# Scan work of VectorE set between projections, two half products of the output in the last chunk of pb, and weight loads in 8 KB rows

## The chip, the cores and the metric

One Trainium2 chip, one core of it. The metric is the device time of one execution in microseconds. The kernel before ran three times: 902.72, 903.78 and 906.15 us, median 903.78.

## What is computed

One encoder block on 256 tokens of width 2048, in float32. The input is normalised, multiplied by one wide matrix (2048 x 13312), and the columns feed a bidirectional linear recurrence (RG-LRU), windowed attention with grouped heads, the gates of both, and two merge gates:

```python
xn = rms_norm(x, norm_pre_w)
z = xn @ w_in
u_lru, g_lru, q, k, v, g_attn, m_lru, m_attn = split(z)
u = centred_depthwise_conv(u_lru, conv_w, conv_b)          # 4 taps
h = rg_lru(u, forward weights) + rg_lru(u, reverse weights)  # h[t] = a[t] h[t-1] + b[t]
y_a = h * silu(g_lru)
y_b = windowed_gqa(rope(q), rope(k), v, sink) * silu(g_attn)
merged = sigmoid(m_lru) * (y_a @ w_proj_a) + sigmoid(m_attn) * (y_b @ w_proj_b)
out = x + rms_norm(merged @ w_out, norm_post_w)
```

## The kernel before, in words

**Products.** Each float32 matrix is used as the sum of a high and a low part. A weight tile comes from DRAM as raw float32, ScalarE (ACT) casts it to the high part `wh` (L230), VectorE (DVE) subtracts that from the raw to get the low part `wl` (L232), and TensorE (PE) makes three products: high by high, low by high, high by low. Where 256 tokens lie side by side, two of them run as one matmul of 512 columns (L263) and the low one as 256 columns (L261); elsewhere all three have 512 columns (L236 to L238, `mm3`).

**Steps and ticks.** The program is a list of steps (`load_plan`), one for each 1 MB of weights (128 x 2048). A step has two halves of 128 x 1024. The kernel is written out half by half: with half `hs`, ACT's cast of half hs+4 and VectorE's split of half hs+3 are issued. The raw tiles of a step are loaded three steps ahead (`fetch`, lead 3). A tick is one half of a normal step or both halves of a `part` step. Everything else hangs on ticks: `at(tick, fn)`, `behind(tick, fn)` (at the end of that tick) and `soon(fn)` (one tick later). The engines each run their instructions in that order, and SP issues nearly all the loads in that order too; a load that must wait for its buffer or its data holds up every load behind it on SP.

**Buffers.** `unit` gives one of UNITS = 50 buffers of 4 KB a partition to everything: raw tiles, wh, wl, activations, gates. A buffer comes free when its last reader is done, whichever engine that is.

**Seven products instead of eight.** Half of the columns of three matrices (groups L, A and O: two merge gates and the output projection) are computed by a Strassen-like scheme of seven products m1 to m7 (`class Seven`), with sums of blocks of activations (`x_sums`, `sums_of`) and sums of blocks of weights. Products m1 and m2 take weights as they are; the others take them from a cell x (m5, then m6, then m4) or y (m3, then m7), in which the next weight block is added onto what is there by an accumulating DMA that POOL issues (L203, queue q0). The next accumulation has to wait until the earlier content is cast and split. In groups L and A the sums of activations are stored to DRAM (`away`, L341) and read back (`Lm`, `Am`, x_sum).

**RG-LRU.** `lru_pair(n, b)` sets the work of two column blocks on ticks from b on: convolution taps (L659), gates, decays, `gi * th` (L726), four scans of 256 steps, two forward and two reverse (L703, L704), `gate_out` (L709, L710) and `y_parts`. The table LRU gives b for each of the eight pairs, XSUM the ticks of the eight `x_sums`.

**The end.** After the projections q, pa, ma and pb (MERGE) comes the output projection (OUT): chunks o2 and o3 as normal steps, the other half as group O (`Om` in the profile). When a chunk of the output is there, `o_done` squares, sums and scales it; at the end the rows of x (`xr`) are added. Weights of the norm are `np`. Attention needs `mask` and `rope`.

The lines that set the order of the tail:

```python
b, n = ticks(), ticks(len(plan))        # b: first tick of OUT, n: last
at(b + 12, load_tail)                   # np
at(n - 6, load_rows)                    # xr
for q in range(2):
    at(b - 16 + 4 * q, lambda q=q: seven.start("x", q))
    at(b - 12 + 4 * q, lambda q=q: seven.second(q))
    at(b - 4 + 4 * q, lambda q=q: seven.start("y", q))
```

Of the kernel before, what the change touches and what calls it, by code (L numbers as in the profile page):

```python
# [29 lines left out]
UNITS = 50  # L30
# [3 lines left out]
G = 1  # L34
# [30 lines left out]
XSUM = (24, 30, 36, 42, 48, 54, 60, 65)  # L65
LRU = (12, 28, 45, 62, 78, 93, 108, 121)
# [62 lines left out]
def body(ctx, tc, x, xT, wall, wlru, pvec, npost, ident_d, mask_d, rope_d, out):  # L129
    nc = tc.nc  # L130
    const = ctx.enter_context(tc.tile_pool(name="const", bufs=1))
    units = ctx.enter_context(tc.tile_pool(name="units", bufs=UNITS))
    small = ctx.enter_context(tc.tile_pool(name="small", bufs=2))
# [136 lines left out]
    def add_rows(name, act, done, spare=False, last=False):  # L270


        got, held = [], []

        def products(t, g, h, wh, wl):
            ts = slice(t * P, (t + 1) * P)
            for j in range(2):
                k = 4 * g + 2 * h + j
                sl = slice(j * 512, (j + 1) * 512)
                a = act[k // 2][:, k % 2, :, ts]  # L280
                mm3(got[t], a[:, 0], a[:, 1], wh[:, sl], wl[:, sl], k == 0, k == KT - 1)

        def half(g, h, wh, wl):
            if g == 0 and h == 0:
                if spare:
# [63 lines left out]
    class Seven:  # L349
# [51 lines left out]
        def half(self, m, q, h, wh, wl):  # L401
            b = {"m6": "m1", "m7": "m1", "m4": "m1", "m3": "m5"}.get(m, m)
# [10 lines left out]
        def keep(self, key, ps):  # L413
            t = self.kept.get("t")
            if key == "u" or t is None:
                t = unit(f"{self.name}{key}", F32, (P, 2, 512))
                if key != "u":
                    self.kept["t"] = t
            self.kept[key] = t[:, int(key == "m5")]
            nc.scalar.copy(self.kept[key], ps)  # L420

        def after(self, m):
# [31 lines left out]
    mask = const.tile([P, 2, S], F32, name="mask")  # L454
    rope = const.tile([ROT, 2, S], F32, name="rope")
# [4 lines left out]
    raw_units(0)  # L460
# [3 lines left out]
    for i in (1, 2):  # L464
        for j in (0, 2):
            nc.sync.dma_start(xt[i][:, j:j + 2], xT[i, :, j:j + 2])
            if j == 0:
                raw_units(i)
# [69 lines left out]

    def load_tables():
        nc.sync.dma_start(mask, mask_d)  # L540
        nc.sync.dma_start(rope, rope_d)

    at(20, load_tables)
# [91 lines left out]
    def lru_pair(n, b):  # L635
# [64 lines left out]
        def scans():  # L700
            a, h, b = v["a"], v["gr"], v["gi"]
            for j in range(2):
                nc.vector.tensor_tensor_scan(h[:, j], a[:, j], b[:, j], 0.0, ALU.mult, ALU.add)  # L703
                nc.vector.tensor_tensor_scan(h[:, 2 + j, ::-1], a[:, 2 + j, ::-1], b[:, 2 + j, ::-1], 0.0, ALU.mult, ALU.add)  # L704
# [25 lines left out]
        at(b + 21 + G, y_parts)  # L730

# [45 lines left out]
    add_ml = lambda c: add_rows(f"ml{c}_", xs, gate_evac(tm, c), c == 0)  # L777
# [19 lines left out]
    swap = [(i + 16) % 32 for i in range(32)]  # L797

    def add_heads(name, then):
# [12 lines left out]
        def rotate(n, d):  # L812
            t = v[n]
            r = t[0:ROT]
            if d == 0:
                v["s"] = small.tile([ROT, 2, S], F32, tag="upad", name=f"{name}s{n}", bufs=2)
                nc.vector.stream_shuffle(v["s"], r, swap)
                nc.vector.tensor_tensor(r, r, rope[:, 0].unsqueeze(1).to_broadcast([ROT, 2, S]), ALU.mult)
            elif d == 1:
                s = v["s"]  # L820
                nc.vector.tensor_tensor(s, s, rope[:, 1].unsqueeze(1).to_broadcast([ROT, 2, S]), ALU.mult)
# [24 lines left out]
    def head(hd, qh, ql, b, both):  # L846
# [11 lines left out]
        def expo():  # L858
# [4 lines left out]
            for t in range(2):  # L863
                nc.vector.tensor_tensor_reduce(p[:, t], sc[:, t], mask[:, t], rtok_sc[:, t:t + 1], sk, ALU.add, ALU.max, m[:, t:t + 1])  # L864
# [59 lines left out]
    def add_pa(c):  # L924
        add_rows(f"pa{c}_", ya, lambda t, ps: nc.vector.tensor_tensor(tm[c][:, t], ps, tm[c][:, t], ALU.mult))
# [39 lines left out]

    tick = add_all(MERGE, lambda kind, c: {
# [4 lines left out]
    }[kind]())  # L971
    for n in range(8):
        at(tick["b0.0"] - 10 + 2 * n, lambda n=n: yb_parts(n))
# [20 lines left out]
    at(b + 12, load_tail)  # L994
    at(n - 6, load_rows)
# [38 lines left out]
    def rows_in_psum():  # L1034

        a, b = banks("xp", (P, 2, 512)), banks("xq", (P, 2, 512))
        xp.update({1: a[:, 0], 3: a[:, 1], 2: b[:, 0]})
# [3 lines left out]
    def o_sum(t, c, ps, other, sign):  # L1041
        if other is None:
            o_done(t, c, ps)
        else:
            f = small.tile([P, 512], F32, tag="p", name=f"of{t}{c}", bufs=2)
# [3 lines left out]
    seven = Seven("O", ms, msum, o_sum)  # L1049
# [4 lines left out]
    add_all(OUT, lambda _, c: add_rows(f"o{c}_", ms, lambda t, ps: o_done(t, c, ps), c == 3, c == 3))  # L1054
# [98 lines left out]
```

## Time and profile before

| | |
|---|---|
| median of three runs | 903.78 us |
| the profiled execution | 906.24 us |
| its span, first to last instruction | 904.5 us |
| granted TensorE clock, mean | 0.993 |
| TensorE busy | 889.1 us |
| VectorE busy | 699.3 us |
| ScalarE busy | 597.6 us |
| moved by DMA | 205.80 MB, mean 228 GB/s |

Times in the profile are microseconds from the start of the span. In lists of waits each row names who waited for whom, then the total, how often, and the longest. In timelines a row gives the start, the duration, the engine, the line and what was written from what; in square brackets stands the idle time ahead of it and what ended that.

### The profile page before, as it was taken

Reading aid. Unit: us, or ns where it says so; the run is one execution under the profiler, and the core shown is the slowest. Engines: PE = TensorE matmul, PEld = TensorE weight load, DVE = VectorE, ACT = ScalarE, POOL = GpSimd, SP = SyncE. Lnnn points to the kernel's source line nnn. Section 1 sums busy time; section 2 is a strip of 40 time slices with the busy share of each in tenths; the row PEclk is TensorE's granted clock in tenths of the full one; section 3 lists DMA queues with packets and bytes.
Section 4 is the critical chain, followed back from the end, with each engine's and each line's share of the span. In section 5 each row is a group of like instructions: output and inputs, shape, how many; then the busy total and the mean of one; then the engine's idle time right before and its main releaser. Section 6 shows DMA issues by size and latency. Waiting matters only on the chain.

```text
span 904.5 us, 12540 instructions
## 1 busy us (share of the span) xinstructions
PE 889.1 (98%) x4590; PEld 760.2 (84%) x4590; DVE 699.3 (77%) x958; ACT 597.6 (66%) x869; POOL 44.7 (5%) x72
## 2 busy tenths in 40 slices
PE   8999999998999999999999999999999999999996
PEld 8888888887888888898888888888888888888865
DVE  6887999798897979798657768586666678668584
ACT  7689695867878788975454555455696565446572
POOL 0000000100010100000000000000001200001100
PEclk9999999999999999999999999999999999999989
DMA  9953476985898956545554554556959987965992
GB/s 326 409 198 111 140 283 214 345 253 193 249 255 304 247 195 219 201 163 209 183 204 150 186 166 139 178 169 215 269 160 323 296 273 221 351 267 140 274 328 96
DMA packets 61646, 205.80 MB, mean 228 GB/s; under 512 B 6512, under 2 KB 11376, under 8 KB 61584
## 3 DMA queue, kind: packets, MB, share of 16 engines
q1 hardware_dynamic: 54096, 179.07, 55.4%
q0 software_dynamic: 6912, 25.17, 14.6%
q8 instruction: 36, 0.59, 0.3%
q10 hardware_dynamic: 576, 0.76, 0.3%
q14 instruction: 26, 0.21, 0.1%
HBM read 198.68 MB, written 6.29 MB: 227 GB/s over the span
## 4 chain that ended last, share of the span: by engine, by line
PE 88%; DMA 6%; DVE 3%; issue 2%; ACT 1%; POOLq 0%; ACTq 0%; SPq 0%; DVEq 0%
PE q L263 6%; PE ga L263 6%; PE gl L263 6%; PE u L263 4%; DMA raw<-wall_dram 4%; PE q L261 3%; PE ga L261 3%; PE gl L261 3%; PE u L261 2%; PE k L263 2%; PE Am L236 1%; PE Am L237 1%; PE Am L238 1%; PE u_ps L555 1%; PE Lm L237 1%
## 5 line engine op out<-in xcount | busy, mean ns | idle before, releaser
L232 DVE TENSOR_TENSOR wl<-raw,wh 128x1024 fp32r<-128x1024 f32 (+1 forms) x276 | 327.7, 1203 | 67.7 <-ACT wh L230 58.0
L230 ACT CAST wh<-raw 128x1024 fp32r<-128x1024 f32 (+1 forms) x275 | 276.2, 1038 | 54.6 <-DMA raw<-wall_dram 33.5
L263 PE MATMUL ga<-xs,wh 128*128 128x512 f32 x256 | 64.2, 398 | 0.0
L263 PE MATMUL q<-xs,wh 128*128 128x512 f32 x256 | 62.8, 391 | 0.0
L263 PE MATMUL gl<-xs,wh 128*128 128x512 f32 x256 | 62.4, 391 | 0.0
L263 PEld LDWEIGHTS ga<-xs,wh 128*128 128x128 f32 x256 | 47.9, 193 | 9.3
L263 PEld LDWEIGHTS gl<-xs,wh 128*128 128x128 f32 x256 | 47.0, 188 | 9.0
L263 PEld LDWEIGHTS q<-xs,wh 128*128 128x128 f32 x256 | 46.6, 188 | 8.8
L263 PE MATMUL u<-xs,wh 128*128 128x512 f32 x192 | 46.8, 391 | 0.0
L160 ACT CAST ph<-pt 128x512 fp32r<-128x512 f32 x16 | 9.4, 586 | 55.2 <-PE pt L884 55.2
L263 PEld LDWEIGHTS u<-xs,wh 128*128 128x128 f32 x192 | 35.2, 188 | 6.7
L261 PE MATMUL ga<-xs,wl 128*128 128x256 f32 x256 | 34.8, 285 | 2.8 <-DVE wl L232 2.8
L261 PEld LDWEIGHTS ga<-xs,wl 128*128 128x128 f32 x256 | 33.3, 191 | 4.8 <-DVE wl L232 3.6
L261 PE MATMUL q<-xs,wl 128*128 128x256 f32 x256 | 34.4, 284 | 0.0
L261 PEld LDWEIGHTS q<-xs,wl 128*128 128x128 f32 x256 | 33.1, 191 | 1.3
L261 PEld LDWEIGHTS gl<-xs,wl 128*128 128x128 f32 x256 | 32.9, 191 | 1.2
L261 PE MATMUL gl<-xs,wl 128*128 128x256 f32 x256 | 33.4, 283 | 0.0
L864 DVE CUSTOM_DVE_ANT_0 p<-sc,mask,pv 128x256 f32<-128x256 f32 x32 | 16.1, 540 | 18.7 <-PE sc L238 18.7
L261 PEld LDWEIGHTS u<-xs,wl 128*128 128x128 f32 x192 | 24.7, 191 | 0.9
L261 PE MATMUL u<-xs,wl 128*128 128x256 f32 x192 | 25.1, 283 | 0.0
L659 DVE SCALAR_TENSOR_TENSOR uu<-upad,pv,uu 128x256 f32<-128x256 f32 x48 | 23.1, 481 | 1.9 <-ACT uu L655 0.2
L160 ACT CAST ms<-mt 128x512 fp32r<-128x512 f32 x8 | 4.7, 588 | 28.5 <-PE mt L942 28.5
(495 smaller groups left out, 2200.6 us busy)
## 6 DMA issues: line engine op xcount, KB each, us to landing
raw<-wall_dram SPq DMA_DIRECT2D x268, 512.0 KB, 5.8
lraw<-wlru_dram SPq DMA_DIRECT2D x8, 512.0 KB, 6.7
away<-xx SPq DMA_DIRECT2D x8, 512.0 KB, 4.1
Lm<-away SPq DMA_DIRECT2D x8, 512.0 KB, 7.6
Am<-away SPq DMA_DIRECT2D x8, 512.0 KB, 10.6
raw<-wall_dram SPq DMA_DIRECT2D x8, 256.0 KB, 4.8
xr<-x_dram SPq DMA_DIRECT2D x4, 512.0 KB, 9.6
Lx0a<-wall_dram POOLq DMA_DIRECT2D x3, 512.0 KB, 8.7
```

The source lines that it names most:

```text
L160: nc.scalar.copy(h, src)
L230: cast(hs, raw)
L232: nc.vector.tensor_tensor(ls, raw, hs.bitcast(F32), ALU.subtract)
L236: nc.tensor.matmul(ps, wh, xh, start=start, stop=False, skip_group_check=more)
L237: nc.tensor.matmul(ps, wh, xl, start=False, stop=False, skip_group_check=more)
L238: nc.tensor.matmul(ps, wl, xh, start=False, stop=stop, skip_group_check=more)
L261: nc.tensor.matmul(ps[:, 1], wl[:, sl], a[:, 0], start=False, stop=False)
L263: nc.tensor.matmul(ps, wh[:, sl], a, start=k == 0, stop=k == KT - 1)
L555: nc.tensor.matmul(ups[b // 2][:, b % 2, m], w[:, sl], a[:, n], start=k == 0 and w is wh and m == 0, stop=stop)
L659: nc.vector.scalar_tensor_tensor(u, up[:, j, tap:tap + S], cw[:, tap:tap + 1], u, ALU.mult, ALU.add)
L864: nc.vector.tensor_tensor_reduce(p[:, t], sc[:, t], mask[:, t], rtok_sc[:, t:t + 1], sk, ALU.add, ALU.max, m[:, t:t + 1])
```

## The change

1. The work of a pair of the RG-LRU after the decays moves to later ticks and is spread: `gi * th` at +19 (17 before), two scans at +21 and two at +24 (all four at +18 before), gate_out at +28 (20), y_parts at +29 (22). LRU changes by one or two ticks for some pairs, XSUM runs from 20 to 55 in steps of 5 (24 to 65 in steps of mostly 6).
2. Raw weight tiles come from a pool of their own, three tiles of 1 MB, each loaded by one DMA with rows of 8 KB instead of two with rows of 4 KB. UNITS goes from 50 to 45.
3. Om1.0 and Om5.0 move into pb's last chunk, and the rest of OUT is reordered. Group O's first x loads start at b-22 and b-14, their second content at b-18 and b-10, its y loads at b-2 and b+2. `np` is loaded at b-8 and `xr` at b-4.
4. m4 gets a PSUM bank of its own in groups A and O: m7's bank is copied aside (`keep("w")`, one ACT copy), and for m4 a combination on VectorE adds it.
5. Gates of the merge wait in DRAM for their use (`park`, four stores of 512 KB, and `back`, four loads). `mask` and `rope` are loaded into a unit six ticks ahead of the heads. `yb_parts` are spread by 1.5 instead of 2 ticks from b0-4 (b0-10 before). Chunk o3 and xp use banks of other pools, and o2's `o_done` comes one and two ticks later.

```diff
-UNITS = 50
+UNITS = 45
...
-G = 1
...
-    b0.3 Am6.1 b1.0 b1.1 Am7.0 b1.2 Am7.1 b1.3 b2.0 Am4.0 b2.1 Am4.1 b2.2 b2.3 b3.0 b3.1 b3.2 b3.3""".split()
-OUT = """o2.0 Om1.0 o2.1 Om1.1 o2.2 Om5.0 Om5.1 o2.3 Om3.0 Om3.1 Om6.0 Om6.1 o3.0 Om2.0 Om2.1 Om7.0 Om7.1 o3.1
-    Om4.0 Om4.1 o3.2 o3.3""".split()
+    b0.3 Am6.1 b1.0 b1.1 Am7.0 b1.2 Am7.1 b1.3 b2.0 Am4.0 b2.1 Am4.1 b2.2 b2.3 b3.0 Om1.0 b3.1 Om5.0 b3.2 b3.3""".split()
+OUT = """o2.0 o2.1 Om1.1 o2.2 Om5.1 Om2.0 o2.3 Om3.0 Om6.0 Om3.1 o3.0 Om6.1 Om2.1 o3.1 Om7.0 Om7.1 Om4.0 Om4.1
+    o3.2 o3.3""".split()
...
-XSUM = (24, 30, 36, 42, 48, 54, 60, 65)
-LRU = (12, 28, 45, 62, 78, 93, 108, 121)
+XSUM = (20, 25, 30, 35, 40, 45, 50, 55)
+LRU = (12, 28, 45, 64, 79, 94, 109, 121)
...
+    ring = ctx.enter_context(tc.tile_pool(name="ring", bufs=3))
...
-    def raw_units(i):
-        raws[i] = [unit(f"raw{i}_{h}", F32, (P, 1024)) for h in range(2)]
-        return raws[i]
+    def raw_tile(i):
+        t = ring.tile([P, 2, 1024], F32, tag="raw", name=f"raw{i}", bufs=3)
+        raws[i] = [t[:, h] for h in range(2)]
+        return t
...
-            load(raw_units(i), plan[i])
+            nc.sync.dma_start(flat(raw_tile(i)), wall[row[content(plan[i])]])
...
+            self.bank = {"m6": "m1", "m7": "m1", "m4": "m1" if sums is None else "m4", "m3": "m5"}
...
                 done(1, 1, ps["m1"], kept["m5"], -1)
+                if self.bank["m4"] == "m4":
+                    self.keep("w", ps["m1"])
             elif m == "m4":
-                done(1, 0, ps["m1"], None, 1)
+                done(1, 0, ps[self.bank["m4"]], kept.get("w"), 1)
...
-            (10, lambda: decays("th", AF.Tanh, cpos, 0)), (10, lambda: decays("th", AF.Tanh, cpos, 1)), (10, gated),
-            (11, lambda: decays("a", AF.Exp, cneg, 0)), (12, lambda: decays("a", AF.Exp, cneg, 1)),
-            (12, lambda: nc.scalar.activation(v["gr"], v["a"], AF.Square)), (13, scale1),
-            (14, lambda: nc.scalar.activation(v["th"], v["th"], AF.Sqrt)),
-            (16, lambda: nc.vector.tensor_tensor(v["gi"], v["gi"], v["th"], ALU.mult)),
-            (17, scans), (19, gate_out),
+            (10, lambda: decays("th", AF.Tanh, cpos, 0)), (10, lambda: decays("th", AF.Tanh, cpos, 1)), (11, gated),
+            (12, lambda: decays("a", AF.Exp, cneg, 0)), (13, lambda: decays("a", AF.Exp, cneg, 1)),
+            (13, lambda: nc.scalar.activation(v["gr"], v["a"], AF.Square)), (14, scale1),
+            (15, lambda: nc.scalar.activation(v["th"], v["th"], AF.Sqrt)),
+            (19, lambda: nc.vector.tensor_tensor(v["gi"], v["gi"], v["th"], ALU.mult)),
+            (21, lambda: scans(0)), (24, lambda: scans(1)), (28, gate_out), (29, y_parts),
         ):
-            at(b + d + (G if d > 5 else 0), fn)
-        at(b + 21 + G, y_parts)
+            at(b + d, fn)
...
+    def park(gates, c):
+
+        d = parked[c] = dram.tile([P, 1024], F32, name=f"park{c}")
+        nc.sync.dma_start(d, flat(gates.pop(c)))
+
+    def back(gates, c):
+        nc.sync.dma_start(flat(gate_unit(gates, c)), parked[c])
...
-    at(b + 12, load_tail)
-    at(n - 6, load_rows)
+    at(b - 8, load_tail)
+    at(b - 4, load_rows)
...
-        at(b - 16 + 4 * q, lambda q=q: seven.start("x", q))
-        at(b - 12 + 4 * q, lambda q=q: seven.second(q))
-        at(b - 4 + 4 * q, lambda q=q: seven.start("y", q))
+        at(b - 22 + 8 * q, lambda q=q: seven.start("x", q))
+        at(b - 18 + 8 * q, lambda q=q: seven.second(q))
+        at(b - 2 + 4 * q, lambda q=q: seven.start("y", q))
```

How the order of instructions moves, at three places. First VectorE around the scans of the first pair (`gr`, `a`, `gi` belong to the pair, `uu` and `upad` to the convolution of the next one, `wl` are splits of raw weights). Before:

```order
L232 TENSOR_TENSOR wl_0_978<-raw_0_916,wh_0_977 128x1024
L703 SCALAR_TENSOR_TENSOR gr_728<-a_856,gi_729 128x256
L704 SCALAR_TENSOR_TENSOR gr_728<-a_856,gi_729 128x256
L703 SCALAR_TENSOR_TENSOR gr_728<-a_856,gi_729 128x256
L704 SCALAR_TENSOR_TENSOR gr_728<-a_856,gi_729 128x256
L659 SCALAR_TENSOR_TENSOR uu_971<-upad_463,pv,uu_971 128x256 x3
L232 TENSOR_TENSOR wl_1_1006<-raw_1_917,wh_1_1005 128x1024
```

Changed (L701 and L702 are the scans, L233 the split, L343 and L324 to L326 the x sums):

```order
L233 TENSOR_TENSOR wl_1_1041<-raw_945,wh_1_1040 128x1024
L701 SCALAR_TENSOR_TENSOR gr_680<-a_837,gi_681 128x256
L702 SCALAR_TENSOR_TENSOR gr_680<-a_837,gi_681 128x256
L589 TENSOR_TENSOR sg_724<-gl_958,sg_724 128x512
L585 TENSOR_TENSOR sg_724<-sg_724,rbc 128x512
L233 TENSOR_TENSOR wl_0_1066<-raw_1001,wh_0_1065 128x1024
L233 TENSOR_TENSOR wl_1_1092<-raw_1001,wh_1_1091 128x1024
L739 TENSOR_TENSOR sg_724<-sg_724,sig_1127 128x512
L233 TENSOR_TENSOR wl_0_1130<-raw_1060,wh_0_1129 128x1024
```

The four scans stood between two splits; now two stand there, and the other two follow four splits later.

Second, the loads on SP in the first third of the program, with the engines they wait for (DMAHW are earlier DMAs; PE_49 means a wait for TensorE). Before:

```order
L205 DMA raw_0_1206<-wall_dram 128x1024 [waits DMAHW7_49,PE_49]
L205 DMA raw_1_1207<-wall_dram 128x1024 [waits DMAHW0_49,PE_49]
L205 DMA raw_0_1281<-wall_dram 128x1024 [waits DMAHW1_49,PE_49]
L205 DMA raw_1_1282<-wall_dram 128x1024 [waits DMAHW2_49]
L341 DMA away_71<-xx_1223 512x1x256 [waits DMAHW3_49,DVE_49]
```

Changed:

```order
L219 DMA raw_1060<-wall_dram 128x2048 [waits DMAHW6_49,DVE_49]
L344 DMA away_74<-xx_1015 512x1x256 [waits DMAHW3_49,DVE_49]
L219 DMA raw_1111<-wall_dram 128x2048 [waits DMAHW7_49,DVE_49]
L219 DMA raw_1182<-wall_dram 128x2048 [waits DMAHW5_49,DMAHW1_49,DVE_49]
L219 DMA raw_1250<-wall_dram 128x2048 [waits DMAHW2_49,DVE_49]
```

A step is one load instead of two, and it waits for VectorE, the last reader of the ring's tile, where it waited for TensorE, the last reader of a unit's former content.

Third, TensorE in pb's last chunk (`pb` are its products, `Om` those of group O). Before:

```order
L237 MATMUL pb__7428<-wl_1_7363,yb_6459 128x512
L238 MATMUL pb__7428<-wh_1_7362,yb_6459 128x512
L236 MATMUL pb__7428<-wh_0_7382,yb_6523 128x512
L237 MATMUL pb__7428<-wl_0_7383,yb_6523 128x512
L238 MATMUL pb__7428<-wh_0_7382,yb_6523 128x512
```

Changed:

```order
L238 MATMUL pb__7199<-wl_1_7138,yb_6401 128x512
L239 MATMUL pb__7199<-wh_1_7137,yb_6401 128x512
L237 MATMUL Om_7256<-wh_0_7155,ms_6746 128x512
L238 MATMUL Om_7256<-wl_0_7156,ms_6746 128x512
L239 MATMUL Om_7256<-wh_0_7155,ms_6746 128x512
```

After the first step of that chunk the twelve matmuls of Om1.0 now stand, and after its second step those of Om5.0, ahead of the output's own chunks.

More of the change, by code (lines that the diff above doesn't have):

```diff
@@ L284, in half @@
             if g == 0 and h == 0:
-                if spare:
+                if last:
+                    got.extend(banks(f"{name}{t}", (P, 2, 512))[:, 0] for t in range(2))
+                elif spare:
                     got.extend(bank(f"{name}{t}", (P, 512)) for t in range(2))
@@ L401, in half @@
         def half(self, m, q, h, wh, wl):
-            b = {"m6": "m1", "m7": "m1", "m4": "m1", "m3": "m5"}.get(m, m)
+            b = self.bank.get(m, m)
             fresh, last = q == 0 and h == 0 and b == m, q == 1 and h == 1
@@ L459, in body @@
     xs = []
-    raw_units(0)
+    raw_tile(0)
     for j in range(4):
@@ L698, in scale1, with scans @@
             nc.vector.scalar_tensor_tensor(v["th"], v["gr"], 1.0, v["th"], ALU.add, ALU.mult)
-        def scans():
+        def scans(j):
             a, h, b = v["a"], v["gr"], v["gi"]
-            for j in range(2):
-                nc.vector.tensor_tensor_scan(h[:, j], a[:, j], b[:, j], 0.0, ALU.mult, ALU.add)
-                nc.vector.tensor_tensor_scan(h[:, 2 + j, ::-1], a[:, 2 + j, ::-1], b[:, 2 + j, ::-1], 0.0, ALU.mult, ALU.add)
+            nc.vector.tensor_tensor_scan(h[:, j], a[:, j], b[:, j], 0.0, ALU.mult, ALU.add)
+            nc.vector.tensor_tensor_scan(h[:, 2 + j, ::-1], a[:, 2 + j, ::-1], b[:, 2 + j, ::-1], 0.0, ALU.mult, ALU.add)
         def gate_out():
@@ L797, in body, with load_tables @@
     swap = [(i + 16) % 32 for i in range(32)]
+    table = {}
+    def load_tables():
+        t = unit("table")
+        table.update(mask=t[:, 0:2], rope=t[0:ROT, 2:4])
+        nc.sync.dma_start(table["mask"], mask_d)
+        nc.sync.dma_start(table["rope"], rope_d)
+    at(ticks() - 6, load_tables)
     def add_heads(name, then):
@@ L924, in add_pa, with done @@
     def add_pa(c):
-        add_rows(f"pa{c}_", ya, lambda t, ps: nc.vector.tensor_tensor(tm[c][:, t], ps, tm[c][:, t], ALU.mult))
+        def done(t, ps):
+            nc.vector.tensor_tensor(tm[c][:, t], ps, tm[c][:, t], ALU.mult)
+            if t == 1 and c >= 2:
+                soon(lambda: park(tm, c), 2)
+        add_rows(f"pa{c}_", ya, done)
     def add_pb(c):
@@ L964, in add_all @@
         return tick
+    seven = Seven("O", ms, msum, lambda *a: o_sum(*a))
     tick = add_all(MERGE, lambda kind, c: {
@@ L971, in body @@
     }[kind]())
+    for c in range(4):
+        at(tick[f"p{c}.0" if c < 2 else f"b{c}.0"], lambda c=c: back(tm, c))
     for n in range(8):
-        at(tick["b0.0"] - 10 + 2 * n, lambda n=n: yb_parts(n))
+        at(tick["b0.0"] - 4 + 3 * n // 2, lambda n=n: yb_parts(n))
     npt, xr, yw = [], [[], []], [[], []]
@@ L1034, in rows_in_psum @@
     def rows_in_psum():
-        a, b = banks("xp", (P, 2, 512)), banks("xq", (P, 2, 512))
-        xp.update({1: a[:, 0], 3: a[:, 1], 2: b[:, 0]})
+        xp.update({q: bank(f"xp{q}", (P, 512)) for q in (1, 3, 2)})
         for q, to in xp.items():
```

32 lines of the change are left out of this document (16 added, 16 removed).

## The prediction

> **What bounds the kernel now.** I read the page first: busy shares and granted clock.
>
> ```profile
> span 904.5 us, 12540 instructions
> PE 889.1 (98%) x4590; PEld 760.2 (84%) x4590; DVE 699.3 (77%) x958; ACT 597.6 (66%) x869; POOL 44.7 (5%) x72
> PEclk9999999999999999999999999999999999999989
> DMA  9953476985898956545554554556959987965992
> ```
>
> TensorE is busy for 98% of the span, and the change takes no matmul away. So all that can be won lies where TensorE waits or runs at a lower granted clock. The clock shows one dip in 40 slices; TensorE's list of waits, read stretch by stretch, leads to it and to one more place. The table by 5 us stretches shows both (columns: stretch, then length, busy time with the number of instructions of PE, PEld, DVE, ACT, POOL, granted clock, DMA share, GB/s).
>
> ```profile
> 200.00:205.00 5.00, 4.21 (x18) 2.85 (x17) 4.96 (x7) 1.57 (x2) 0.14 (x2) 1.00 0.63 252
> 205.00:210.00 5.00, 2.76 (x18) 2.46 (x19) 4.46 (x8) 3.43 (x6) 0.00 (x0) 0.91 0.00 0
> 210.00:215.00 5.00, 5.00 (x24) 4.24 (x23) 4.96 (x7) 4.97 (x7) 0.00 (x0) 0.74 0.70 188
> ...
> 860.00:865.00 5.00, 3.35 (x13) 1.97 (x11) 2.35 (x3) 2.20 (x5) 1.33 (x2) 0.95 1.05 276
> 865.00:870.00 5.00, 4.54 (x11) 3.37 (x11) 4.67 (x5) 4.80 (x6) 0.00 (x0) 0.50 1.05 273
> 870.00:875.00 5.00, 5.00 (x20) 4.04 (x20) 4.93 (x9) 3.94 (x6) 0.00 (x0) 0.87 1.04 340
> ```
>
> First place: TensorE idle 0.79 + 2.24 = 3.0 us, VectorE full, and DMA at nothing in the middle stretch. Second: idle 1.65 + 0.46 = 2.1 us, DMA at its limit, and the clock at half for a whole stretch. What each costs I take from TensorE's timeline (start, duration, instruction).
>
> ```profile
> 200.16 0.39 PE L238 MATMUL Lm<-wh,xs 128*128 128x512 f32 x1
> 200.39 0.39 PE L236 MATMUL Lm<-wh,xs 128*128 128x512 f32 x1
> 201.22 0.50 PE L237 MATMUL Lm<-wl,xs 128*128 128x512 f32 x1 [0.45 <-DVE wl L232]
> ...
> 202.48 2.00 PE L263 MATMUL ga<-xs,wh 128*128 128x512 f32 x8
> 204.82 1.21 PE L261 MATMUL ga<-xs,wl 128*128 128x256 f32 x8 [0.34 <-DVE wl L232]
> 208.28 1.39 PE L261 MATMUL ga<-xs,wl 128*128 128x256 f32 x8 [2.24 <-DVE wl L232]
> 209.46 3.45 PE L263 MATMUL ga<-xs,wh 128*128 128x512 f32 x8
> 212.75 0.28 PE L236 MATMUL gate<-ul,lwh 128*128 128x256 f32 x1
> 212.87 0.28 PE L237 MATMUL gate<-ul,lwh 128*128 128x256 f32 x1
> ...
> 861.01 0.39 PE L236 MATMUL Om<-wh,ms 128*128 128x512 f32 x1
> ...
> 871.41 0.40 PE L238 MATMUL Om<-wh,mx 128*128 128x512 f32 x1
> 871.65 0.40 PE L236 MATMUL Om<-wh,mx 128*128 128x512 f32 x1
> ```
>
> Unhindered, matmuls of 512 columns start 0.227 us apart (0.23 between the first two rows) and those of 256 columns 0.12. From 200.39 to 212.75 there are 6 of Lm, 16 of L263 and 16 of L261: 22 x 0.227 + 16 x 0.12 = 6.9 us of work in 12.36 us. **Stall 1 costs 5.4 us.** From 861.01 to 871.65 stand 21 matmuls: 21 x 0.227 = 4.8 in 10.64 us. **Stall 2 costs 5.9 us.** Both fall on VectorE's low parts (wl) or what feeds them. The causes differ. VectorE ahead of stall 1, then SP's list of waits over the span (total, times, longest), then a piece of the chain that ended stall 1:
>
> ```profile
> 192.41 1.22 DVE L232 TENSOR_TENSOR wl<-raw,wh 128x1024 fp32r<-128x1024 f32 x1
> 193.54 0.68 DVE L703 TENSOR_TENSOR_SCAN gr<-a,gi 128x256 f32<-128x256 f32 x1
> ...
> 195.31 0.67 DVE L704 TENSOR_TENSOR_SCAN gr<-a,gi 128x256 f32<-128x256 f32 x1
> 195.89 1.57 DVE L659 SCALAR_TENSOR_TENSOR uu<-upad,pv,uu 128x256 f32<-128x256 f32 x3
> 197.38 1.22 DVE L232 TENSOR_TENSOR wl<-raw,wh 128x1024 fp32r<-128x1024 f32 x1
> ...
> 204.68 0.69 DVE L340 TENSOR_TENSOR xa<-xs 128x512 f32<-128x512 f32 x1
> ...
> 206.40 0.68 DVE L161 TENSOR_TENSOR ul<-uu,ul 128x512 fp32r<-128x512 f32 x1
> 207.00 1.22 DVE L232 TENSOR_TENSOR wl<-raw,wh 128x1024 fp32r<-128x1024 f32 x1
> ```
>
> ```profile
> SPq L341 <- DVE xx L161: 94.3, 8, 18.7
> ```
>
> ```profile
> 174.61 6.28 DMA raw<-wall_dram
> ```
>
> From the split at 192.41 to that at 207.00 VectorE passes four half steps (197.38, 199.95, 203.55 and 207.00 are their splits) in 14.6 us, where TensorE takes 12 x 0.227 = 2.72 us for one, 10.9 in all. It falls behind by 3.7 us, and it was behind already: the raw tile awaited from 174.61 to 180.9 came late, and SP, which starts these loads in program order, had stood in front of `away` stores (L341) for up to 18.7 us. Four scans in a row (193.54 to 195.89, 2.35 us), taps, gi x th and the x sums fall into one stretch.
>
> For stall 2: a piece of its chain, the first of the last twelve accumulations in POOL's timeline, and queues and issues between 832 and 868 us.
>
> ```profile
> 845.02 18.30 DMA raw<-wall_dram
> ```
>
> ```profile
> 825.55 0.86 POOL L203 DMA_DIRECT2D Ox0a<-wall_dram  x1 [44.01 <-DVE wl L232]
> ```
>
> ```profile
> q0 software_dynamic: 1343, 4.91, 68.5%
> q1 hardware_dynamic: 1344, 4.92, 36.4%
> ...
> raw<-wall_dram SPq DMA_DIRECT2D x10, 512.0 KB, 12.7
> ```
>
> Packets of both queues are equal in number and bytes in these 36 us: they take turns. An accumulating packet lasts 0.685 x 36 x 16 / 1343 = 0.294 us, a loading one 0.156. Raw weights get 4.92 MB / 36 us = 137 GB/s, one step (1 MB) in 7.7 us, while TensorE finishes a full step in 2 x 2.72 = 5.4. The accumulations had been held back (POOL waits 44 us for Om5.0's split) and then run as one block; a raw load takes 12.7 us, in the chain 18.3.
>
> **The change part by part.** *Scans in two pairs, gi x th at +19, LRU and XSUM tables.* VectorE's work stays the same, it is spread. By the order of the changed kernel, the stretch with the taps, the x sums and the first pair of scans has six half steps from the end of one split to the end of the sixth: taps 1.5, x sums 1.7 (204.68 to 206.40), ul and xx 1.3, gi x th and lwl 2.3, two scans 1.2, the gate path's three 512-wide steps 2.0: 10.0 us, and six splits of 1.13 are 6.8. That is 16.8 us against TensorE's 6 x 2.72 = 16.3: 0.5 us behind instead of 3.7, and the split runs three half steps ahead. Gain: 5.4, all of stall 1. Bounds: nothing (raw loads are late again) to 5.4. I take 5.4, because the loads no longer wait for activations to leave their buffers (next part). Its cover is the lead of three half steps; gone, up to 0.5 us per pair, eight pairs, 4 us.
>
> *Raw tiles in a ring of three, one load of 1 MB.* A load waits for the second split of the step three back, and TensorE needs it about six and a half half steps later by the order: 18 us, less one cast and one split, 15.8. What lands in 5.8 us now, as 512 KB, is covered:
>
> ```profile
> raw<-wall_dram SPq DMA_DIRECT2D x268, 512.0 KB, 5.8
> ```
>
> Rows of 8 KB are not in the trace of q1. Bounds: two such packets' worth of time for twice the bytes (no gain) or, if turns go by packet, q1 gets twice its share beside q0. By the first the cost is 0; by the second raws gain and accumulations lose: one turn of 0.294 + 2 x 0.156 = 0.61 us then moves 8 KB and 4 KB over 16 engines, 216 and 108 GB/s instead of 146 each, and an accumulation of 512 KB takes 4.9 instead of 3.6 us. I take 0, nearest to both.
>
> The Trainium skill ("DMA: Bandwidth & Descriptors", section "Queues, rings and completion order") says that each DMA engine goes round-robin between the rings at packet granularity; the equal packet counts above agree. By it the second bound holds and the accumulations would lose as computed there.
>
> *Om1.0 and Om5.0 in pb's last chunk, O's starts six ticks earlier, m4 in a bank of its own.* The second set of accumulations into O's x cell (for m6) no longer waits for an Om5.0 behind o2, so the twelve (Ox, Oy) spread from before pb's end to the tail, not one block from 825 on; m4's partner copy lets m4 end without m7's bank. Stall 2 goes: 5.9. Bounds: 0 (the block only moves) to 5.9. I take 5.9, since DMA has room ahead of 825 (digit 5 in the slice from 814, then 9 and 9) and POOL there waited for that split last. The extra copy (0.58) and combination (0.68) are hidden: from 860 to 865 both engines are busy for under half of the time. If that cover goes, they cost 1.3. From ACT's and VectorE's timelines, the same operations:
>
> ```profile
> 855.90 0.58 ACT L420 COPY Ou<-Om 128x512 f32<-128x512 f32 x1
> ```
>
> ```profile
> 857.17 0.68 DVE L758 SCALAR_TENSOR_TENSOR of<-Om,Ou 128x512 f32<-128x512 f32 x1
> ```
>
> *Parked gates:* 4 writes and 4 reads of 0.52 MB, 4.2 MB; at the 273 GB/s of both queues 15 us of DMA, spread over stretches whose DMA digits in the page (tenths of a slice of 22.6 us) are mostly 4 to 6. Cost 0; if one lands in front of each raw load with no slack, 1.9 us each, 15 in all; that needs landings already at 15.8. Behind a `park` on SP wait the raw loads of the next steps; it waits for gates two ticks old. Tables, np and xr loads move earlier: xr leaves the crowded tail.
>
> *New small waits:* the most VectorE work between two splits stands, by the changed order, at the k steps, about 4.1 us (an estimate from the durations of the same operations before) where 2.72 - 1.13 = 1.6 fits a half step: 2.5 behind, still inside three half steps. I allow 1.0 in all.
>
> **Sum.** The profiled run took 906.24 us (span 904.5 and 1.7 around it): 906.24 - 5.4 - 5.9 + 1.0 = 895.9. It lies 2.5 us above the median of the runs shown. If that belongs to the stalls, a changed run comes out at 895.9; if not, at 893.4. I take the middle, **894.5 us** against 903.78, about -1.0%.
>
> **The clock, and what the skill says against it.** In stall 1 the longest single wait is 2.24 us, in stall 2 all of them together make 2.1, yet the clock fell to 0.74 and 0.50. The missing clock is (0.09 + 0.26) x 5 = 1.8 and (0.05 + 0.50 + 0.13) x 5 = 3.4 us: 5.2 of the 11.3 us. The Trainium skill ("TensorE: Matmul & The Clock Gate", section "What's actually happening") has the gate fall only after an idle window of some 3.4 us. By that rule the dips would not come from these waits, and could stay when the waits go. As a mechanism here: the waits go, the dips stay, 894.5 + 5.2 = 899.7. The rows speak against it: outside the start, the clock drops only at the two waits; chance 0.03.
>
> **The rivals.**
> - *One stall stays or a like one comes* (raws late at the scans; or accumulations squeezed by 8 KB rows: twelve lose 1.3 us each, 16 us, against slack of two ticks and their pauses; the last comes some 3 us late, and 2 us of clock go with it). 894.5 + 5.4 = 899.9. For it: DMA is at its limit from 860 on (share 1.05), and the bytes stay the same. Against: 44 us of waiting become usable. Chance 0.15, with the clock's 0.03 together 0.18.
> - *The spread work only shifts the late splits*: at the k steps and again behind pb, 11 us of new waits. 905. For it: VectorE at 77%. Against: 16.8 in 16.3 us above. Chance 0.08.
> - *The ring is too shallow.* Slower: a 1 MB load that needs the 18.3 us of the chain row, against 15.8, is 2.5 us late; there are 12 bundles of four accumulations (three groups: L, A, O). It decides from 15.8 us to landing. From seven bundles on it outweighs the gain: eight give 894.5 + 20 = 914. For it: before has 50 units to lend, after has three tiles. Against: 5.8 us as a rule. Chance 0.06.
> - *More goes than the two stalls*, the small waits from 500 to 850 us too: 890. Chance 0.04.
> The forecast keeps 0.64.
>
> **How the numbers follow.** The forecast's own range is 892 to 897 (893.4 and 895.9 with the 1.0 either way). With the case of one stall (to 901) it holds 0.82; left out are 0.08, 0.06 and 0.04. So 891 to 901. A measurement tells 0.5% (4.5 us) from no change: under 899.3 is faster. Of the one-stall case (899.9) under half falls there: 0.64 + 0.04 + 0.08 = 0.76 faster; 0.10 + 0.08, less a little that goes beyond, 0.17 the same; 0.07 slower.
>
> **What would show it.** No wait of a TensorE row on wl over 0.5 us between 190 and 220 us, clock 1.00 there; TensorE full and the clock at 1.00 from 840 to 875; POOL's second set of Ox accumulations starting before 820, with pauses between the sets; raw landings (1 MB) under 12 us. Wrong: raw landings at or above 15.8, TensorE waiting for ACT's cast of raw, a new wait at the k steps (385 to 400 us), or a clock below 1.00 without a wait ahead of it.

## The result, and the profile after

| | before | after |
|---|---|---|
| median of four runs, us | 903.55 (902.72 to 906.15) | 894.36 (893.97 to 894.69) |
| profiled execution, us | 906.24 | 894.46 |
| its span, us | 904.5 | 892.7 |
| mean granted clock | 0.993 | 0.997 |

The ratio is 0.9893, with a 95% interval from 0.9873 to 0.9914: the kernel is 1.1% faster. The prediction was 894.5, its range 891 to 901.

The page of the changed kernel, the lines that answer to those of before:

```profile
span 892.7 us, 12161 instructions
...
PE 883.7 (99%) x4590; PEld 758.2 (85%) x4590; DVE 698.5 (78%) x959; ACT 600.4 (67%) x870; POOL 44.8 (5%) x72
...
PEclk9999999999999999999999999999999999999998
DMA  9766667897797946365555444546979987799962
```

The list of TensorE's waits over the whole span has a single row left, from the warm-up matmuls at the start:

```profile
PE spin L458 <- POOL eps L454: 1.0, 1, 1.0
```

The stretches of the two places (length, then busy PE, PEld, DVE, ACT, POOL, clock, DMA share, GB/s). The second lies earlier than before, since the changed kernel is ahead by 6 us there:

```profile
200.00:205.00 5.00, 5.00 (x30) 4.42 (x29) 4.96 (x6) 4.29 (x5) 0.14 (x2) 1.00 0.48 159
205.00:210.00 5.00, 5.00 (x29) 4.35 (x29) 5.00 (x8) 3.48 (x4) 0.00 (x0) 1.00 0.64 233
...
850.00:855.00 5.00, 5.00 (x23) 4.14 (x23) 3.08 (x3) 0.63 (x1) 0.49 (x1) 1.00 1.03 283
855.00:860.00 5.00, 5.00 (x23) 4.13 (x23) 3.38 (x4) 4.94 (x9) 0.38 (x1) 1.00 1.05 295
860.00:865.00 5.00, 5.00 (x23) 4.13 (x22) 4.93 (x9) 4.50 (x5) 0.00 (x0) 1.00 0.57 112
```

VectorE is as full as before around 205 us, and DMA as full from 850 to 860, but TensorE never waits and the clock stays at 1.00. The busy share of an engine that is not the bound says little here; the waits that end last say more.

Where the time went: counted by matmuls (the traces of both kernels hold 4590 TensorE instructions, so the n-th of one can be set beside the n-th of the other), the changed kernel is ahead by 0.2 us at the 950th (173 us), 5.6 at the 1250th (232 us), 6.1 at the 1650th (304 us), 6.1 at the 4300th (825 us) and 12.1 at the 4500th (876 us). So stall 1 gave 5.4, a small wait near 299 us gave 0.5, stall 2 gave 6.0, and nothing in between gave or took anything. Behind the last matmul 0.3 us are lost. These sizes are those of two executions, which lie 11.8 us apart in time; the medians lie 9.2 us apart.

POOL's timeline shows the accumulations of the tail; the second Ox set begins at 788.50 and not at 825.55. Only its first two accumulations lie that early; the other ten are issued from 821.32 to 855, with one long pause (9.8 us) among them:

```profile
788.50 0.86 POOL L204 DMA_DIRECT2D Ox0a<-wall_dram  x1 [13.40 <-DVE wl L233]
789.63 0.89 POOL L204 DMA_DIRECT2D Ox0b<-wall_dram  x1 [0.27 <-issue]
821.32 0.88 POOL L204 DMA_DIRECT2D Ox1a<-wall_dram  x1 [30.80 <-DVE wl L233]
823.06 0.86 POOL L204 DMA_DIRECT2D Ox1b<-wall_dram  x1 [0.86 <-DVE wl L233]
833.73 0.87 POOL L204 DMA_DIRECT2D Oy0a<-wall_dram  x1 [9.81 <-DVE wl L233]
```

### The profile page after: what moved, and what is told of

The parts are those of the page before. It is cut to its first block, busy times and chain, and to the rows that moved or that the text cites. A ratio compares the mean times of both kernels' runs of the same rounds, so it can differ in the third digit from the quotient of the medians.

```text
span 892.7 us, 12161 instructions
## 1 busy us (share of the span) xinstructions
PE 883.7 (99%) x4590; PEld 758.2 (85%) x4590; DVE 698.5 (78%) x959; ACT 600.4 (67%) x870; POOL 44.8 (5%) x72
## 4 chain that ended last, share of the span: by engine, by line
PE 93%; issue 4%; DMA 2%; DVE 0%; POOLq 0%; ACTq 0%; POOL 0%; DVEq 0%
PE q L264 7%; PE gl L264 7%; PE ga L264 7%; PE u L264 5%; PE ga L262 3%; PE gl L262 3%; PE q L262 3%; PE u L262 3%; PE k L264 2%; PE Am L237 1%; PE Am L239 1%; PE Am L238 1%; PE Lm L239 1%; PE Lm L238 1%; PE Lm L237 1%
## 5 line engine op out<-in xcount | busy, mean ns | idle before, releaser
L233 DVE TENSOR_TENSOR wl<-raw,wh 128x1024 fp32r<-128x1024 f32 (+1 forms) x276 | 326.8, 1203 | 63.8 <-ACT wh L231 43.4
L888 DVE CUSTOM_DVE_ANT_0 p<-sc,table,pv 128x256 f32<-128x256 f32 x32 | 16.1, 541 | 13.4 <-PE sc L239 13.4
L681 ACT ACTIVATE gr<-gate,pv 128x256 f32<-128x256 f32 x32 | 15.2, 476 | 11.7 <-PE gate L239 11.7
```

What stands on the lines that cost most here:

```text
L233: nc.vector.tensor_tensor(ls, raw, hs.bitcast(F32), ALU.subtract)
L681: nc.scalar.activation(v["gr"][:, 2 * d + j], ps[:, 0], AF.Sigmoid, bias=pv[:, PV_BR + b:PV_BR + b + 1])
L888: nc.vector.tensor_tensor_reduce(p[:, t], sc[:, t], table["mask"][:, t], rtok_sc[:, t:t + 1], sk, ALU.add, ALU.max, m[:, t:t + 1])
```

## The experiments

Each kernel was compared with the kernel before on the same chip. Medians of before were 904.86 for the first four runs, 905.57 for the next four and 904.81 for the last four. Two questions were open, one for each stall: which part of the change removes it. No run takes out the parked gates, the early `mask` and `rope` or the new `yb_parts` alone.

### Stall 1: place, tables or loads

`before_new_scans`: the kernel before with the new ticks and tables alone (the other ticks of a pair as in the change).

```diff
-XSUM = (24, 30, 36, 42, 48, 54, 60, 65)
-LRU = (12, 28, 45, 62, 78, 93, 108, 121)
+XSUM = (20, 25, 30, 35, 40, 45, 50, 55)
+LRU = (12, 28, 45, 64, 79, 94, 109, 121)
...
-            (17, scans), (19, gate_out),
+            (21, lambda: scans(0)), (24, lambda: scans(1)), (28, gate_out), (29, y_parts),
```

> The kernel before with the new ticks of the RG-LRU pairs and the new LRU and XSUM tables, and nothing else of the change (4 KB rows, 50 units, old tail). Scan theory (stall 1 comes from VectorE's work standing in one heap): stall 1 goes, stall 2 stays; about 898 us (897 to 899.5), no TensorE wait on wl over 0.5 us between 195 and 215 us. Load theory (stall 1 comes from raw tiles that arrive late, because units wait for TensorE and SP stands in front of other work): at least 3 us of stall 1 stay, 901 us or more.

Measured: 898.07 us, ratio 0.9931 (0.9915 to 0.9948). Stretches of its trace:

```profile
200.00:205.00 5.00, 5.00 (x31) 4.42 (x30) 4.96 (x7) 4.19 (x5) 0.14 (x2) 1.00 1.02 404
205.00:210.00 5.00, 5.00 (x30) 4.36 (x29) 5.00 (x7) 3.47 (x4) 0.00 (x0) 1.00 0.11 43
```

Stall 1 is gone with the old units and the old loads. The load theory falls.

`after_old_scans`: the changed kernel with the old ticks and tables (the reverse of the diff above; the gates of a pair come one tick later again too).

> The changed kernel with the old ticks of the RG-LRU pairs (all four scans at +18) and the old LRU and XSUM tables; ring, 8 KB rows and tail as changed. Scan theory: stall 1 comes back, about 900 us (899 to 902), TensorE waiting for wl around 195 to 205 us. Load theory (the ring's even loads give enough lead): no stall or under 1.5 us, 894.5 to 896 us.

Measured: 899.43 us, ratio 0.9937 (0.992 to 0.9954), 5 us above the changed kernel. Its waits of TensorE between 195 and 215 us, then two stretches:

```profile
PE ga L262 <- DVE wl L233: 2.6, 2, 2.2
PE Lm L238 <- DVE wl L233: 0.5, 1, 0.5
```

```profile
205.00:210.00 5.00, 2.76 (x14) 2.46 (x13) 4.50 (x8) 4.05 (x6) 0.00 (x0) 0.69 0.29 77
210.00:215.00 5.00, 5.00 (x22) 4.28 (x21) 4.96 (x7) 4.96 (x8) 0.00 (x0) 0.63 0.97 326
```

The same waits, in the same place, as before the change: 2.2 us the longest, busy 2.76 of 5 us. The ring does not protect against them. With the run above, cause and cure are shown both ways: it is the order of the pairs' work and of the x sums, whatever the loads.

`before_new_ticks`: as `before_new_scans`, but with the old LRU and XSUM tables.

> The kernel before with the new ticks of the RG-LRU pairs, but with its own LRU and XSUM tables. If the spread of the scans alone does it: 898 us, as before_new_scans. If the x sums that fall beside the second pair (XSUM 54, 60, 65) are the larger part: stall 1 stays at 2 us or more, 900 to 903 us.

Measured: 898.3 us, ratio 0.9931 (0.9906 to 0.9957). Between 190 and 220 us one wait of 0.4 us is left, of a gate product. The ticks are enough; the tables add a few tenths of a us at most. XSUM, and with it the time at which SP comes to the `away` stores, is as before here.

`after_four_scans`: all four scans of a pair at +21.

```diff
-            (21, lambda: scans(0)), (24, lambda: scans(1)), (28, gate_out), (29, y_parts),
+            (21, lambda: scans(0)), (21, lambda: scans(1)), (28, gate_out), (29, y_parts),
```

> The changed kernel with all four scans of a pair at +21, not two at +21 and two at +24. If it is the place beside the taps and gi x th that made the heap, four in a row (2.35 us) fit there: 894.4 us, no wait on wl. If it is the run of four as such: at least 2 us of waits near 195 to 215 us, 896.5 us or more.

Measured: 894.21 us, ratio 0.9882 (0.9867 to 0.9897), no wait on a split. So setting the scans in two pairs is not what helps. Nor is it the distance from the next pair's taps (`uu`): the four scans stand right between them.

```profile
195.28 1.59 DVE L658 SCALAR_TENSOR_TENSOR uu<-upad,pv,uu 128x256 f32<-128x256 f32 x3
196.79 1.22 DVE L233 TENSOR_TENSOR wl<-raw,wh 128x1024 fp32r<-128x1024 f32 x1
197.92 0.69 DVE L701 TENSOR_TENSOR_SCAN gr<-a,gi 128x256 f32<-128x256 f32 x1
...
199.69 0.67 DVE L702 TENSOR_TENSOR_SCAN gr<-a,gi 128x256 f32<-128x256 f32 x1
200.27 1.50 DVE L658 SCALAR_TENSOR_TENSOR uu<-upad,pv,uu 128x256 f32<-128x256 f32 x3
```

What differs is how much work of VectorE stands there in all. From one split to the fifth behind it TensorE takes 5 x 2.72 = 13.6 us. VectorE took 18.8 us before (from the split at 188.19 to that at 207.00) and 18.8 in `after_old_scans` (187.57 to 206.38), and there TensorE waits. It took 16.3 in `before_new_ticks` (188.47 to 204.78) and at most 14.6 here (191.87 to 206.43), and there TensorE waits for no split. With the lead of three half steps, 2.7 us behind does no harm and 5.2 does. How far behind VectorE may fall between the two was not measured.

### Stall 2: order, rows or loads

`before_new_tail`: the kernel before with the new MERGE and OUT order, the new starts of group O's cells, and m4's bank with what goes with it.

```diff
-        at(b - 16 + 4 * q, lambda q=q: seven.start("x", q))
-        at(b - 12 + 4 * q, lambda q=q: seven.second(q))
-        at(b - 4 + 4 * q, lambda q=q: seven.start("y", q))
+        at(b - 22 + 8 * q, lambda q=q: groups["O"].start("x", q))
+        at(b - 18 + 8 * q, lambda q=q: groups["O"].second(q))
+        at(b - 2 + 4 * q, lambda q=q: groups["O"].start("y", q))
```

> The kernel before with the new MERGE and OUT order, the new starts of group O's cells, m4 in its own bank and the banks and delays that go with it; raw loads stay two of 4 KB rows, xr and np are loaded at their old places, scans stay. Block theory (stall 2 comes from the accumulations held back and then run in one block): stall 2 goes, stall 1 stays; about 898 us (897 to 899.5). Row theory (it comes from equal turns of packets, and 8 KB rows give the raws their share; or from xr in the tail): stall 2 stays, 902 us or more.

Measured: 900.68 us, ratio 0.9956 (0.9941 to 0.9971). In its trace no TensorE wait is left behind 310 us: stall 2 is gone. The time is above the expected 898. A part of that may be a longer wait near 299 us, which the profiled execution shows (902.29 us, the slowest of the six), between 295 and 303:

```profile
PE ga L261 <- DVE wl L232: 2.6, 1, 2.6
```

Before, that wait was 0.2 us in the profiled execution. Whether the other five have it isn't known.

`after_old_tail`: the changed kernel with the old order and the old starts (the reverse of the diff above, and of MERGE and OUT; m4 keeps its own bank).

> The changed kernel with the old MERGE and OUT order and the old starts of group O's cells; xr and np loads stay early, ring and 8 KB rows stay. Block theory: stall 2 comes back at 5 to 6 us, about 900 us, TensorE idle and clock near 0.5 around 850 to 860 us. Row theory: little of it comes back, 895 to 896 us.

Measured: 894.37 us, ratio 0.9888 (0.9873 to 0.9903). **No stall comes back.** Against the block theory, which the prediction had, the new order isn't needed in the changed kernel. Its accumulations stand in one block from 819 us on, as before.

`after_units`: raw tiles back in common units (51 of them), two loads of 4 KB rows.

```diff
-UNITS = 45
+UNITS = 51
...
-        t = ring.tile([P, 2, 1024], F32, tag="raw", name=f"raw{i}", bufs=3)
-        raws[i] = [t[:, h] for h in range(2)]
-        return t
+        raws[i] = [unit(f"raw{i}_{h}", F32, (P, 1024)) for h in range(2)]
+        return raws[i]
```

> The changed kernel with raw tiles in 51 common units again, two loads of 4 KB rows to a step. Scan and block theory: no stall comes back, 894.5 us (894 to 895.5). Load theory and row theory: one of the stalls comes back, 898 us or more.

Measured: 895.1 us, ratio 0.9895 (0.9881 to 0.991). That is 0.7 us above the median of the changed kernel, and no wait of TensorE is left behind the start: with the new order, the ring isn't needed either.

So either the order or something else among ring, rows and loads is enough. Three runs with the old order tell which. `after_old_tail_4k` loads each ring tile with two DMAs of 4 KB rows:

```diff
-            nc.sync.dma_start(flat(raw_tile(i)), wall[row[content(plan[i])]])
+            raw_tile(i)
+            load(raws[i], plan[i])
```

> As after_old_tail, but each ring tile is loaded by two DMAs of 4 KB rows. Row theory (with 8 KB rows the raw queue moves twice the bytes in each turn beside the accumulations: 207 against 105 GB/s between 851 and 860 us of after_old_tail): without them stall 2 comes back, 897 to 900 us. Early-rows theory (np and xr out of the tail are what keeps the block harmless): no stall, 894 to 895 us.

Measured: 894.12 us, ratio 0.9884 (0.9854 to 0.9915). The row theory falls: 4 KB rows do as well. `after_old_tail_late` keeps 8 KB rows and loads np and xr at their old places, `after_old_tail_np_late` only np:

```diff
-    at(b - 8, load_tail)
-    at(b - 4, load_rows)
+    at(b + 12, load_tail)
+    at(n - 6, load_rows)
```

> As after_old_tail, with np and xr loaded at their old late places; the ring and 8 KB rows stay. Row theory: no stall, 894 to 895 us. Early-rows theory: stall 2 comes back in part or whole, 896 to 900 us.

> As after_old_tail, with only np back at its old late place; xr stays early, rows are 8 KB. Queue theory: the first of the two stalls of after_old_tail_late (3.5 us near 855 us) comes back with an SP wait in front of np, 897 to 899 us. If xr makes both stalls: none, 894 to 895 us.

Measured: 900.7 us, ratio 0.9948 (0.9928 to 0.9968), and 898.24 us, ratio 0.9929 (0.9914 to 0.9944). With np late, SP stands in front of it; its list of waits between 770 and 870 us in `after_old_tail_np_late`:

```profile
SPq L1015 <- DVE wl L233: 9.9, 1, 9.9
SPq L1015 <- PE Om L239: 7.6, 1, 7.6
```

L1015 is the load of np: 17.5 us in which no raw load behind it starts. With xr late too, a second stall follows near 875 us (xr late alone was not run). There the casts wait for accumulations; ACT's list of waits in `after_old_tail_late`, 840 to 885 us:

```profile
ACT wh L231 <- DMA raw<-wall_dram: 9.6, 3, 3.6
ACT wh L231 <- DMA Ox0b<-wall_dram: 3.9, 1, 3.9
```

`before_early_rows`: the kernel before with np and xr early, and nothing else (the reverse of the diff above).

> The kernel before with np loaded at b-8 and xr at b-4, and nothing else of the change. Queue theory (stall 2 begins where SP stands 13.3 us in front of np, with raw loads behind it and the DMA engines idle, and the block of accumulations only keeps the delay from being made up): stall 2 goes, stall 1 stays, 897 to 900 us. Block theory as first told (the block alone makes the raws late): stall 2 stays, 903 us or more.

Measured: 904.17 us, ratio 0.9996 (0.9978 to 1.0015): no change. Stall 2 stays, and the queue theory in its simple form (np alone) falls. SP still stands, now in front of raw loads whose units are not free; its longest rows between 805 and 850 us:

```profile
SPq L205 <- DVE wl L232: 22.0, 4, 11.5
SPq L205 <- PE Om L238: 14.4, 3, 6.9
```

What the kernels with a stall have in common is seen in the load of the DMA engines just ahead of the block of accumulations. Stretches 814 to 822 and 822 to 830 us, first the kernel before, then `before_early_rows`, `after_old_tail_np_late` and `after_old_tail`:

```profile
814.00:822.00 8.00, 8.00 (x39) 6.63 (x38) 7.28 (x12) 6.68 (x10) 0.00 (x0) 1.00 0.37 133
822.00:830.00 8.00, 8.00 (x37) 6.64 (x36) 6.93 (x8) 5.13 (x6) 2.62 (x3) 1.00 0.34 58
```

```profile
814.00:822.00 8.00, 8.00 (x39) 6.61 (x38) 7.28 (x13) 6.05 (x11) 0.00 (x0) 1.00 0.55 195
822.00:830.00 8.00, 8.00 (x37) 6.63 (x36) 6.94 (x8) 5.14 (x7) 1.75 (x2) 1.00 0.20 41
```

```profile
814.00:822.00 8.00, 8.00 (x37) 6.60 (x36) 6.94 (x8) 5.13 (x7) 1.75 (x2) 1.00 0.14 17
```

```profile
814.00:822.00 8.00, 8.00 (x37) 6.64 (x36) 6.92 (x8) 5.67 (x8) 1.75 (x2) 1.00 0.86 281
822.00:830.00 8.00, 8.00 (x37) 6.64 (x36) 6.11 (x6) 3.75 (x4) 2.59 (x3) 1.00 1.02 195
```

The last but one number of a row is the DMA share. The three kernels with a stall have a hole there, 0.14 to 0.37 of the DMA engines in use for at least 8 us, while SP stands and raw loads are still to be issued; the one without uses 0.86 and more. In `after_old_tail_late` the share is 0.09 from 814 to 822. `after_old_tail_4k` is like the last (0.76 from 814 on). `before_new_tail` has such a hole too (0.16 from 822 to 830) and no stall: there the accumulations pause for 10 us (from 832 to 842). That raw loads catch up in this pause is read from the one trace and not tested apart.

### The ring's depth

`after_ring_of_two`: two ring tiles, 47 units, raw loads two steps ahead in the program.

```diff
-    ring = ctx.enter_context(tc.tile_pool(name="ring", bufs=3))
+    ring = ctx.enter_context(tc.tile_pool(name="ring", bufs=2))
...
-        if lead == 3 and i not in raws and not chained(i):
+        if lead == 2 and i not in raws and not chained(i):
```

> The changed kernel with two ring tiles instead of three (47 units, raw loads two steps ahead; the third tile of the start in units). A raw load then has about two half steps less, some 10 us from the split that frees its tile to the cast. If the ring's depth is what carries the raw loads: casts wait for raws where POOL's accumulations run (landings there 7.5 us and more), 898 to 910 us. If raw loads have room to spare: within 1 us of 894.4.

Measured: 927.3 us, ratio 1.0252 (1.0227 to 1.0277), 33 us above three tiles. ACT's list of waits over the span, here first and in the changed kernel second:

```profile
ACT wh L234 <- DMA raw<-wall_dram: 188.0, 71, 11.2
```

```profile
ACT wh L231 <- DMA raw<-wall_dram: 24.4, 12, 5.6
```

One of its stalls (TensorE waits 3.2 us at 287 us) is preceded by this piece of the chain:

```profile
271.32 18.18 DMA raw<-wall_dram
```

A raw load that takes 18 us does occur, and two tiles don't cover it. The changed kernel, with three, has none so long: its longest takes 15.1 us, issued near 250 us, and TensorE doesn't wait for it. Longer ones occur with three tiles too: in `after_old_tail_late` one of 25 us stands in the chain ahead of the first stall. First the load of the changed kernel (the last number is the time from issue to landing), then that piece of the chain:

```profile
raw<-wall_dram SPq DMA_DIRECT2D x1, 1024.0 KB, 15.1
```

```profile
828.69 25.01 DMA raw<-wall_dram
```

The run with two tiles changes depth and lead together, so it doesn't split the 33 us between them.

## Why the prediction was right, point by point

**The bound.** TensorE's matmuls, and two stalls in them. Right: matmul by matmul, 5.4 and 6.0 us came from those two places in the profiled executions, against 5.4 and 5.9 in the sum.

**Stall 1, the term of 5.4.** Mechanism and size right, shown both ways. The reckoning of 16.8 us of VectorE's work in 16.3 us of TensorE's did not hold in its items: six half steps, from the split at 193.91 to that at 209.67, took 15.8 us, the x sums that it counts with 1.7 us stand elsewhere, and the second pair of scans falls into the stretch. The end is the same, no wait on a split. The reason given for taking the whole 5.4, that loads no longer wait for activations, was not needed: `before_new_scans` and `before_new_ticks` have the old loads and no stall, and `after_old_scans` has the ring and the stall. And the pairs of scans don't count, but the sum of the work that stands between the splits.

**Stall 2, the term of 5.9.** The size was right, the reason too narrow. The step that failed is "I take 5.9, since DMA has room ahead of 825 (digit 5 in the slice from 814, then 9 and 9) and POOL there waited for that split last", that is, the gain put down to the new order alone. The digit 5 that was read as room is the hole itself: for 13.3 us of that slice SP stands in front of np, with the raw loads behind it. In every run with this stall two things stand together: raw loads that stop for 8 us or more ahead of the accumulations, because SP stands in front of np or of a unit that isn't free, and accumulations in one block behind. The new order breaks up the second; the changed kernel's loads with early np remove the first. Either is enough. Those loads with np and xr late (`after_old_tail_late`) are not, and np and xr early in the kernel before (`before_early_rows`) are not. What in the changed kernel keeps SP moving stays open in part: `before_early_rows` and `after_old_tail` differ in the ring, but also in the parked gates, the scans and the banks, and no run has the old order, early np and common units in the changed kernel. The prediction saw that xr leaves the crowded tail, and gave no weight to np at the head of SP's queue.

**8 KB rows, costed at nothing.** Right for the time (894.37 with, 894.12 without, both with the old order). The share was as worked out from equal turns. The queues of `after_old_tail` between 851 and 860 us:

```profile
q0 software_dynamic: 262, 0.95, 52.9%
q1 hardware_dynamic: 258, 1.86, 51.3%
```

Equal numbers of packets, and q1 moves twice the bytes: 207 against 106 GB/s (1.86 and 0.95 MB in 9 us), where 216 and 108 were worked out. That agrees with the rule of turns by packet in the Trainium skill ("DMA: Bandwidth & Descriptors", section "Queues, rings and completion order"). Where xr comes late as well, accumulations are what the casts wait for (3.9 us above). In the changed kernel no wait of TensorE comes of it.

**New waits, 1.0.** There were none; instead the wait of 0.5 near 299 us went, and 0.3 was lost behind the last matmul. On the basis of the profiled execution the forecast was 895.9, and 894.46 came. The forecast of 894.5 was about the middle between that and 893.4 (exactly, 894.65). That it hit to 0.1 us is luck, two errors that cancel: the middle took off some 1.3 us too much, since the 2.5 us by which the profiled execution lay above the median seem to have belonged to the stalls (after the change the profiled execution lies 0.1 above its median), and the allowance and the wait near 299 us made the sum some 1.5 us too high. Parked gates, costed at nothing, were not run apart.

**The clock.** The dips went with the waits, and in `after_old_scans` they came back with them: waits of 2.2 us at most, and the clock at 0.69 and 0.63. But waits don't always bring a dip. In `after_old_tail_np_late` TensorE waits 0.76 + 1.35 us in two stretches of 845 to 860 and the clock stays at 1.00:

```profile
845.00:850.00 5.00, 4.24 (x18) 2.78 (x17) 2.89 (x3) 1.99 (x2) 0.86 (x1) 1.00 1.04 311
...
855.00:860.00 5.00, 3.65 (x14) 2.15 (x12) 2.99 (x4) 4.07 (x6) 0.88 (x1) 1.00 1.03 310
```

`before_new_scans` has the tail of the kernel before, and TensorE idle for 2.45 us in one stretch of its stall 2; the clock stays at 1.00, where it fell to 0.50 before after 2.1 us:

```profile
855.00:860.00 5.00, 2.55 (x10) 1.23 (x9) 2.90 (x3) 2.47 (x4) 0.86 (x1) 1.00 1.06 274
```

And `before_early_rows` has a smaller dip in its stall 2:

```profile
865.00:870.00 5.00, 3.13 (x11) 2.02 (x10) 2.69 (x4) 3.92 (x6) 0.00 (x0) 0.93 1.06 283
870.00:875.00 5.00, 5.00 (x18) 3.96 (x17) 5.00 (x5) 3.74 (x5) 0.00 (x0) 0.73 0.86 269
```

Added up as the prediction does, the missing clock is (0.07 + 0.27) x 5 = 1.7 us here, 1.8 in stall 1 and 3.4 in stall 2 of the kernel before, (0.31 + 0.37) x 5 = 3.4 in `after_old_scans`, and nothing in `before_new_scans`. So in these traces a stall loses no clock, some 1.7 us or some 3.4, and its size is that of one execution. The rule that the gate falls only after an idle window of some 3.4 us (the Trainium skill, "TensorE: Matmul & The Clock Gate", section "What's actually happening") doesn't hold as it stands for stall 1, whose longest wait is 2.24 us. What decides here stays open.

**The rivals.** The shallow ring is a mechanism for slower that two tiles show (927.3 us); three are deep enough for what the changed kernel asks of them. None of the others came. Of the signs that the prediction named, one did not come: raw landings were to stay under 12 us, and the longest takes 15.1, under the 15.8 that it named as a sign of being wrong.

## What to carry to other kernels

Before a stall is put down to the transfer that is slow in it, look at the DMA engines in the 30 to 50 us ahead (the hole from 814 to 830 us stands that far ahead of the stall at 861 in the kernel before): if they are idle there while loads are due, see whether the load queue is standing in front of something; in the stalls here it was. On a queue that starts loads in program order, a small load whose buffer isn't free holds up all that waits behind it (17.5 us here). And with an engine that runs three half steps ahead, add up all its work from one split to the fifth behind it: four scans in a row (2.35 us) did no harm, 5 us more than TensorE's time did.

## What the runs showed that was not expected

The waits near 299 us differ between profiled executions: 0.2 us in that of before, 1.4 in that of `before_early_rows`, 2.6 in that of `before_new_tail`; in kernels with the new ticks there is none, and none in `after_old_scans` either, which has the old ones. The runs of before spread over 3.4 us (902.72 to 906.15), those of the changed kernel over 0.7: with the waits most of the spread went too. The granted clock goes with that spread: of the 41 executions of before beside the later runs, those with a mean clock of 0.997 or more took 900.83 to 905.67 us, those with 0.993 took 905.56 to 909.45. That the waits cause the spread, by the dips that they bring or don't bring, wasn't tested apart.

With 8 KB rows both queues together moved 312 GB/s (2.81 MB in 9 us between 851 and 860 us of `after_old_tail`), where 4 KB rows gave 273 in the tail of before.
